# First stage of a two-block transformer kernel: scale, spreading of c and sums of squares moved to TensorE, first weights laid out by input block

## Chip, cores and metric

The kernel runs as one program on one core of a Trainium2 chip. The metric is the time of one execution on the device in microseconds (us); the span of a profile runs from its first to its last instruction.

## What is computed

A first block of two layers runs over x (512 positions by 1024 features), then a second block of two layers over the result. Only the start and the end matter here. Each sublayer of the first block normalises x and modulates it by vectors that come from c; the gated feed-forward network follows:

```python
def rmsnorm(x, g):
    y = xf * lax.rsqrt(jnp.mean(xf * xf, axis=-1, keepdims=True) + EPS)
    return y * g
def modulate(x, g, shift, scale):
    return rmsnorm(x, g) * (1.0 + scale[:, None, :]) + shift[:, None, :]
def first_block(...):
    c_act = jax.nn.silu(c)
    mod = (c_act @ w_mod[l] + b_mod[l]).reshape(c.shape[0], N_MOD, D_MODEL)
    h = modulate(x, g_norm[l, 0], mod[:, 0], mod[:, 1])
    x = x + 0.5 * mod[:, 2][:, None, :] * swiglu(h, w_ffn1_gu[l], w_ffn1_down[l])
    ...
```

The second block is modulated in the same way by vectors from c_2 and c_ctx_2, and its last step is a layer norm (mean and variance over the features) of the sum of x and the last feed-forward network; its result is the output.

## The kernel before, in words

**Layout.** x lies transposed: eight tiles of 128 features by 512 positions. A matrix product of fp32 accuracy is made of three fast ones (fp32r): each operand is split into a high half (a cast on ScalarE: wh, hh) and the rest (a subtraction on VectorE: wl, hl), and `mm3` issues high x high, high x low and low x high. A weight block is 128 x 512 (four tiles of 128 x 128, 256 KB); `wblk` loads it (wr) and makes wh and wl. `wcol` takes two blocks, all eight input tiles of one output tile.

**Order of work.** The program is first recorded, operation by operation, with a number each (`Recorder.call`: `prio` is the count of operations so far plus `later`). `Recorder.schedule` then plays all five queues with a cost per instruction (`Recorder.cost`) and lets each engine take the ready operation with the lowest number; the order that comes out is emitted. Loads all go through SyncE's queue and are ordered in the same way. A tag bounds what is under way: at most 8 weight blocks between load and split, 12 between load and last matmul, 8 PSUM banks.

**Start.** `setup` loads the eight x tiles, then `load_c(0, "c")` loads c twice 512 wide, broadcast by the DMA to 128 partitions, and ScalarE applies silu (b_c). `first_mods` makes the shift Sh and the scale G of the first sublayer, one feature chunk m of 128 at a time. Of wmod, transposed on the host so that a row belongs to one output feature, it loads two halves of 128 x 512 for the shift and two for the scale (mr). The dot product with b_c is one VectorE instruction with a running sum for one half of each; for the other half (`FIRST_POOL`) GpSimd multiplies and ScalarE sums. Small VectorE steps add the halves, the bias and the gain. `nc.later = FIRST[0] + FIRST[1] * m` moves the numbers of chunk m by 100 + 16 m; a chunk has 13 operations.

`rms` squares the x tiles on ScalarE (sq), adds the eight tiles on VectorE (`total`, seven adds), sums over partitions by four one-column fp32 matmuls with ones (`colsum`), takes the inverse root by ten small VectorE steps (`rsqrt`) and spreads the row over partitions by four transposes (`bcast`). `modulated` makes for each k: tm (VectorE), hh (ScalarE), hl (VectorE). Then `ffn` goes over pairs p of gate and value: for each of two halves eight input tiles k, 24 matmuls of 512 columns into a PSUM bank, then silu, product and split. `gu_blocks` packs the weights so that a block holds four input tiles of one output tile.

`setup_rest`, recorded after four steps of the first block, calls `load_c` for c_2 and the context's c (b_c2, b_cc). `run` interleaves the main line with `gen_mods`, which makes all other modulation vectors.

**End.** `ln_part` of the last layer (mod is None) works on two halves of 256 positions. Each sums x over the tiles on GpSimd and the squares on VectorE, sums both over partitions by two one-column matmuls each (`colsum`), makes mean and inverse root, spreads them (bm and a PSUM bank), and subtracts, multiplies and stores. The second half's is recorded behind all dense matmuls of the last down projection.

Names in the profile: mr (rows of wmod), b_c, sq, acc (sums of tiles), ones, c (small columns), mods (Sh and G), tm, hh/hl, wr/wh/wl, ps (any PSUM bank). Every operation shows line 446, the place where the planner emits it.

Of the kernel before, what the change touches and what calls it, by code (L numbers as in the profile page):

```python
# [40 lines left out]

def down_blocks():
    return [[(k, m) for m in range(m0, m0 + 4 // len(ch)) for k in ch] for ch in FF_CHUNKS for m0 in range(0, KD, 4 // len(ch))]
# [21 lines left out]
FIRST_POOL = (1, 3)  # L65
# [87 lines left out]
class Recorder:  # L153
# [28 lines left out]
    def cost(self, eng, method, a, k):  # L182
        out = a[0]
        n = out.width() if isinstance(out, View) else a[1].width()
        if eng == "tensor":
            if method == "transpose":
                return 0.84 * n + 2
            x = a[2]
            return max(0.4167 * n, 107) + 13.4 if x.t.dt == F32R else 112
# [281 lines left out]
class Core:  # L471
# [45 lines left out]
    def setup(self):  # L517
# [9 lines left out]
        self.cb = {}  # L527
        self.x = []
# [4 lines left out]
        self.load_c(0, "c")  # L533
# [7 lines left out]
    def load_c(self, i, k):  # L541
        nc = self.nc
        for h in range(2):
            t = self.t(s="b_" + k)
            nc.sync.dma_start(t, self.io["cvec"][i:i + 1, h * 512:(h + 1) * 512].to_broadcast([P, 512]))
            nc.scalar.activation(t, t, AF.Silu)
            self.cb[k, h] = t
# [95 lines left out]
    def first_mods(self):  # L643

        nc = self.nc
        Sh, G = self.mods[:, 0:8], self.mods[:, 8:16]
        for m in range(8):
            nc.later = FIRST[0] + FIRST[1] * m
            dots = []
            for ch in range(2):  # L650
                d = [self.col(1), self.col(1)]
                for h in range(2):
                    raw = self.t(s="mr")
                    nc.sync.dma_start(raw, self.io["wmod"][0, ch * 8 + m][:, h * 512:(h + 1) * 512])
                    if (2 * ch + h) % 4 in FIRST_POOL:
                        nc.gpsimd.tensor_tensor(raw, raw, self.cb["c", h], op=ALU.mult)
                        nc.scalar.activation(raw, raw, AF.Identity, accum_out=d[h])
                        continue
                    nc.vector.scalar_tensor_tensor(raw, raw, 1.0, self.cb["c", h], op0=ALU.mult, op1=ALU.mult, accum_out=d[h])
                dots.append(d)  # L660
            for ch, out in enumerate((Sh, G)):
                nc.vector.scalar_tensor_tensor(out[:, m:m + 1], dots[ch][0], dots[ch][1], self.bmod[:, ch * 8 + m:ch * 8 + m + 1], op0=ALU.add, op1=ALU.add)
            nc.vector.scalar_tensor_tensor(G[:, m:m + 1], G[:, m:m + 1], 1.0, self.gn[:, m:m + 1], op0=ALU.add, op1=ALU.mult)
# [63 lines left out]
    def colsum(self, tiles, T, eng=None, more=0):  # L727
        nc = self.nc
        acc = self.total(tiles, T, eng)
        st = self.ps()  # L730
        for j in range(T // P):
            nc.tensor.matmul(st[:, j:j + 1], acc[:, j * P:(j + 1) * P], self.ones, start=True, stop=True)
# [29 lines left out]
    def rms(self, x, T, width, eps=1e-6):  # L762
# [6 lines left out]
        st, v, q = self.colsum(sq, T, more=2)  # L769
# [24 lines left out]
    def ffn(self, x, h, gu, dn, gate, T, conv=None, before_last=None, head=HEAD, after=None):  # L794
        nc = self.nc
        last = len(FF_CHUNKS) - 1
        for ci, ch in enumerate(FF_CHUNKS):
            hid = []
            for pi, p in enumerate(ch):
                halves = []  # L800
                for half in range(2):
                    ws = self.wcol(gu, 2 * p + half)
                    pg = self.ps()[:, :T]
                    self.lin(pg, ws, h, parts=parts(T) if ci == 0 and 2 * pi + half < head else None)
# [22 lines left out]
        yield from self.ffn_end(x, dn, prev, hid, gate, T, after)  # L827

# [68 lines left out]
    def rms_part(self, l, sub):  # L897
# [3 lines left out]
        def part(sl):  # L901
# [4 lines left out]
            self.modulated(x, self.rms(x, T, D), G, Sh, [(hi[:, sl], lo[:, sl]) for hi, lo in out], T)  # L906
# [305 lines left out]
    def ln_part(self, xs, T, l, which, kind, mod, perm=False):  # L1212
# [8 lines left out]
        def part(sl):  # L1221
# [13 lines left out]
            s1 = self.colsum(x, C, nc.gpsimd)  # L1235
            s2, v, q = self.colsum(sq, C, more=2)
# [499 lines left out]
def layout(i):  # L1736
# [7 lines left out]
    o["wmod"] = np.stack([rowtiles(i["w_mod"][l]) for l in range(DEPTH)])  # L1744
    o["wada"] = np.stack([rowtiles(i["ada_w_2"][l]) for l in range(DEPTH)])
# [24 lines left out]
    for l in range(DEPTH):  # L1770
        o[f"gu1_{l}"] = pack(i["w_ffn1_gu"][l], gu_blocks())
# [70 lines left out]
```

## Time and profile before

| | before |
|---|---|
| median of 3 runs | 3553.25 us (3552.89 to 3555.09) |
| the profiled execution | 3556.54 us |
| its span | 3554.8 us |
| TensorE matmul, busy share | 97% |
| VectorE, ScalarE, GpSimd, busy share | 75%, 51%, 22% |
| share of the chain that ended last: TensorE, VectorE, ScalarE, DMA | 88%, 5%, 3%, 2% |
| TensorE busy in the first and the last of 40 slices | 6 and 8 tenths |

A slice is 88.9 us. Busy shares are averages over the whole span; in a window each column gives the busy time of an engine and, in brackets, its instructions. A matmul's own duration is longer than the distance to the next, because matmuls overlap: distances between starts tell the rate. An fp32 matmul (not fp32r) makes two records in the trace.

### The profile page before, as it was taken

What the parts mean: (1) busy time and instruction counts of PE and PEld (TensorE: products, weight loads), DVE (VectorE), ACT (ScalarE), POOL (GpSimd) and SP (SyncE); (2) the same over time, 40 slices, a digit from 0 to 9 for tenths busy, and PEclk for the clock granted to TensorE, in tenths of its full rate; (3) what the DMA queues carried; (4) which work ended last, traced back from release to release, by engine and by line L of the source; (5) the groups of instructions that cost most, each with busy time, mean ns of one, the idle gap of its engine ahead of it and who ended that gap; (6) DMA issues with size and microseconds to landing.
All of it is one profiled execution on the core that took longest, in us unless ns stands there. A gap on an engine that the chain in (4) does not pass through costs nothing.

```text
span 3554.8 us, 56919 instructions
## 1 busy us (share of the span) xinstructions
PE 3463.3 (97%) x19814; PEld 3046.3 (86%) x19814; DVE 2668.0 (75%) x5556; ACT 1811.8 (51%) x3933; POOL 768.6 (22%) x848
## 2 busy tenths in 40 slices
PE   6999999999999999999999999999999999989998
PEld 5888989888988889898888988888888889988887
DVE  8984689867697658798645699987668767876566
ACT  6443555534555455664333487874445444454333
POOL 4330032322132112223100133350001522240002
PEclk9999999999999999999999999999999999999999
DMA  9874145556376542448535212124343143333330
GB/s 337 293 229 123 58 151 155 184 159 191 104 252 193 163 119 93 117 146 268 180 104 150 87 44 60 57 69 130 106 127 107 54 125 104 91 105 104 97 90 24
DMA packets 276448, 475.37 MB, mean 134 GB/s; under 512 B 40000, under 2 KB 55872, under 8 KB 276160
## 3 DMA queue, kind: packets, MB, share of 16 engines
q1 hardware_dynamic: 276160, 471.74, 43.4%
q8 instruction: 156, 2.56, 0.3%
q14 instruction: 132, 1.08, 0.1%
HBM read 448.81 MB, written 5.50 MB: 128 GB/s over the span
## 4 chain that ended last, share of the span: by engine, by line
PE 88%; DVE 5%; ACT 3%; DMA 2%; issue 1%; POOL 0%; SPq 0%; POOLq 0%; DVEq 0%; ACTq 0%
PE ps L446 88%; DVE wl L446 1%; ACT L446 1%; DVE c L446 0%; DVE x L446 0%; DVE pl L446 0%; ACT pth L446 0%; ACT pl L446 0%; SPq L446 0%; DMA mr<-in_wmod 0%; DVE ptl L446 0%; ACT gt L446 0%; DMA wr<-in_dn 0%; DVE mr L446 0%; ACT pc L446 0%
## 5 line engine op out<-in xcount | busy, mean ns | idle before, releaser
L446 DVE TENSOR_TENSOR wl<-wr,wh 128x512 fp32r<-128x512 f32 (+1 forms) x1182 | 851.9, 741 | 136.8 <-ACT wh L446 100.7
L446 ACT CAST wh<-wr 128x512 fp32r<-128x512 f32 (+1 forms) x1182 | 678.5, 614 | 116.6 <-PE ps L446 65.5
L446 PE MATMUL ps<-hh,wh 128*128 128x512 f32 (+1 forms) x1864 | 687.7, 369 | 4.9 <-ACT hh L446 4.8
L446 PE MATMUL ps<-hh,wl 128*128 128x512 f32 (+1 forms) x1864 | 684.5, 367 | 6.0 <-DVE wl L446 6.0
L446 PE MATMUL ps<-hl,wh 128*128 128x512 f32 (+1 forms) x1864 | 685.4, 368 | 4.4 <-DVE hl L446 4.4
L446 PE MATMUL ps<-fh,wh 128*128 128x512 f32 (+1 forms) x1344 | 464.1, 345 | 0.0
L446 PE MATMUL ps<-fl,wh 128*128 128x512 f32 (+1 forms) x1344 | 461.8, 344 | 0.0
L446 PE MATMUL ps<-fh,wl 128*128 128x512 f32 (+1 forms) x1344 | 461.7, 344 | 0.0
L446 PEld LDWEIGHTS ps<-hh,wl 128*128 128x128 f32 x1864 | 352.2, 189 | 65.6 <-DVE wl L446 7.8
L446 PEld LDWEIGHTS ps<-hh,wh 128*128 128x128 f32 x1864 | 352.6, 189 | 61.7 <-ACT hh L446 5.8
L446 PEld LDWEIGHTS ps<-hl,wh 128*128 128x128 f32 x1864 | 352.5, 189 | 61.2 <-DVE hl L446 6.4
L446 DVE SCALAR_TENSOR_TENSOR x<-ps,mods,x 128x512 f32<-128x512 f32 (+1 forms) x400 | 255.2, 641 | 177.8 <-PE ps L446 173.9
L446 PE MATMUL ps<-ah,wh 128*128 128x512 f32 (+1 forms) x1000 | 367.1, 367 | 2.0 <-ACT ah L446 2.0
L446 PE MATMUL ps<-al,wh 128*128 128x512 f32 (+1 forms) x1000 | 366.1, 366 | 0.2
L446 PE MATMUL ps<-ah,wl 128*128 128x512 f32 (+1 forms) x1000 | 365.7, 366 | 0.0
L446 PEld LDWEIGHTS ps<-fh,wl 128*128 128x128 f32 x1344 | 254.5, 189 | 30.2
L446 PEld LDWEIGHTS ps<-fh,wh 128*128 128x128 f32 x1344 | 254.6, 189 | 29.5
L446 PEld LDWEIGHTS ps<-fl,wh 128*128 128x128 f32 x1344 | 254.7, 190 | 29.3
L446 DVE SCALAR_TENSOR_TENSOR cv<-ps,ffc,cv 128x511 f32<-128x511 f32 (+1 forms) x264 | 172.6, 658 | 140.0 <-ACT cv L446 136.8
L446 POOL TENSOR_TENSOR mr<-mr,b_c 128x512 f32<-128x512 f32 x123 | 182.2, 1484 | 403.2 <-DMA mr<-in_wmod 287.8
L446 ACT ACTIVATE cv<-ps,ffc 128x512 f32<-128x512 f32 (+1 forms) x132 | 93.2, 708 | 323.5 <-PE ps L446 323.0
L446 ACT CAST fh<-s 128x512 fp32r<-128x512 f32 x132 | 81.9, 621 | 276.9 <-DVE s L446 276.9
(332 smaller groups left out, 6947.0 us busy)
## 6 DMA issues: line engine op xcount, KB each, us to landing
wr<-in_gu SPq DMA_DIRECT2D x352, 256.0 KB, 3.3
mr<-in_wmod SPq DMA_DIRECT2D x288, 256.0 KB, 4.4
wr<-in_fin SPq DMA_DIRECT2D x264, 256.0 KB, 2.7
mr<-in_wada SPq DMA_DIRECT2D x192, 256.0 KB, 3.6
wr<-in_dn SPq DMA_DIRECT2D x176, 256.0 KB, 3.1
wr<-in_fout SPq DMA_DIRECT2D x132, 256.0 KB, 2.7
wr<-in_win SPq DMA_DIRECT2D x64, 256.0 KB, 3.1
wr<-in_nqkv SPq DMA_DIRECT2D x48, 256.0 KB, 3.0
```

The source lines that it names most:

```text
L446: getattr(eng, method)(*a, **k)
```

## The change

It makes the first scale on TensorE: wscale is the scale's part of w_mod with 128 input features on the partitions; for each m eight fp32 matmuls with a weight tile of 128 x 128 and one column of silu(c) (ccol) accumulate in a column of one PSUM bank (sums), and one VectorE step makes G. The shift's two products stay on VectorE, both halves. GpSimd and ScalarE have no product of the first stage any more. c is loaded as two rows ahead of x and spread over 128 partitions by fp32 matmuls with a row of ones, for c and, in `setup_rest`, for the two others. `colsum(each=True)` drops the adds and accumulates one-column matmuls of every tile in PSUM: in the first `rms` (8 x 4 matmuls) and in the last half of the last layer norm, for x and for the squares (2 x 8 x 2). The first four gate and value tiles of the first network (pairs 0 and 1) are packed by input block: block k holds input tile k of all four, and `first_pairs` accumulates in four PSUM banks, k by k. The planner's cost of an fp32 matmul of 256 columns or more rises to 1.7 ns a column.

```diff
--- before.py
+++ after.py
@@ -39,6 +39,11 @@
     return [[(k, m) for k in range(k0, k0 + 4)] for p in range(NFF) for m in (p, NFF + p) for k0 in (0, 4)]
 
 
+def first_blocks():
+
+    return [[(k, m) for m in (0, NFF, 1, NFF + 1)] for k in range(KD)] + gu_blocks()[8:]
+
+
 def down_blocks():
     return [[(k, m) for m in range(m0, m0 + 4 // len(ch)) for k in ch] for ch in FF_CHUNKS for m0 in range(0, KD, 4 // len(ch))]
 
@@ -62,7 +67,6 @@
 FIRST = (100, 16)
 HEAVY = 0.5
 FILL, DEBT, STEP = 0.7, 5000.0, 500.0
-FIRST_POOL = (1, 3)
 ON_DVE, ON_DVE_LAST = 1, 1
 BEGIN = 20000.0
 POOLED = (1, 3)
@@ -186,7 +190,7 @@
             if method == "transpose":
                 return 0.84 * n + 2
             x = a[2]
-            return max(0.4167 * n, 107) + 13.4 if x.t.dt == F32R else 112
+            return max(0.4167 * n, 107) + 13.4 if x.t.dt == F32R else 112 if n < 256 else 1.7 * n
         if eng == "sync":
             rows = (out.box[1] - out.box[0]) if isinstance(out, View) else P
             return max(450, rows * n * 4 / 360)
@@ -525,12 +529,13 @@
         nc.vector.memset(mean, 1.0 / D)
         nc.scalar.copy(self.mean, mean)
         self.cb = {}
+        self.firsts = []
+        self.load_c(0, "c")
         self.x = []
         for m in range(KD):
             t = self.t(s="x")
             self.nc.sync.dma_start(t, self.io["xT"][m * P:(m + 1) * P, :])
             self.x.append(t)
-        self.load_c(0, "c")
         self.gn = self.load_const("gnorm")
         self.bmod = self.load_const("bmod")
         self.mods = self.cst([P, 264], "mods")
@@ -540,10 +545,16 @@
 
     def load_c(self, i, k):
         nc = self.nc
+        row = self.new("t", (1, 512), F32, "crow"), self.new("t", (1, 512), F32, "crow")
         for h in range(2):
+            nc.sync.dma_start(row[h], self.io["cvec"][i:i + 1, h * 512:(h + 1) * 512])
+        one = self.new("t", (1, P), F32, "one")
+        nc.vector.memset(one, 1.0)
+        for h in range(2):
+            p = self.ps()
+            nc.tensor.matmul(p, one, row[h], start=True, stop=True)
             t = self.t(s="b_" + k)
-            nc.sync.dma_start(t, self.io["cvec"][i:i + 1, h * 512:(h + 1) * 512].to_broadcast([P, 512]))
-            nc.scalar.activation(t, t, AF.Silu)
+            nc.scalar.activation(t, p, AF.Silu)
             self.cb[k, h] = t
 
     def setup_rest(self):
@@ -644,23 +655,25 @@
 
         nc = self.nc
         Sh, G = self.mods[:, 0:8], self.mods[:, 8:16]
+        up, c = self.col(8), self.col(8)
+        nc.sync.dma_start(c, self.io["ccol"])
+        nc.scalar.activation(c, c, AF.Silu)
+        nc.vector.tensor_scalar(up, self.bmod[:, 8:16], 1.0, None, op0=ALU.add)
+        sums = self.ps()
         for m in range(8):
             nc.later = FIRST[0] + FIRST[1] * m
-            dots = []
-            for ch in range(2):
-                d = [self.col(1), self.col(1)]
-                for h in range(2):
-                    raw = self.t(s="mr")
-                    nc.sync.dma_start(raw, self.io["wmod"][0, ch * 8 + m][:, h * 512:(h + 1) * 512])
-                    if (2 * ch + h) % 4 in FIRST_POOL:
-                        nc.gpsimd.tensor_tensor(raw, raw, self.cb["c", h], op=ALU.mult)
-                        nc.scalar.activation(raw, raw, AF.Identity, accum_out=d[h])
-                        continue
-                    nc.vector.scalar_tensor_tensor(raw, raw, 1.0, self.cb["c", h], op0=ALU.mult, op1=ALU.mult, accum_out=d[h])
-                dots.append(d)
-            for ch, out in enumerate((Sh, G)):
-                nc.vector.scalar_tensor_tensor(out[:, m:m + 1], dots[ch][0], dots[ch][1], self.bmod[:, ch * 8 + m:ch * 8 + m + 1], op0=ALU.add, op1=ALU.add)
-            nc.vector.scalar_tensor_tensor(G[:, m:m + 1], G[:, m:m + 1], 1.0, self.gn[:, m:m + 1], op0=ALU.add, op1=ALU.mult)
+            for h in range(2):
+                raw = self.t(s="mg")
+                nc.sync.dma_start(raw, self.io["wscale"][m][:, h * 512:(h + 1) * 512])
+                for j in range(4):
+                    nc.tensor.matmul(sums[:, m:m + 1], raw[:, j * P:(j + 1) * P], c[:, 4 * h + j:4 * h + j + 1], start=h == 0 and j == 0, stop=h == 1 and j == 3)
+            nc.vector.scalar_tensor_tensor(G[:, m:m + 1], sums[:, m:m + 1], up[:, m:m + 1], self.gn[:, m:m + 1], op0=ALU.add, op1=ALU.mult)
+            d = [self.col(1), self.col(1)]
+            for h in range(2):
+                raw = self.t(s="mr")
+                nc.sync.dma_start(raw, self.io["wmod"][0, m][:, h * 512:(h + 1) * 512])
+                nc.vector.scalar_tensor_tensor(raw, raw, 1.0, self.cb["c", h], op0=ALU.mult, op1=ALU.mult, accum_out=d[h])
+            nc.vector.scalar_tensor_tensor(Sh[:, m:m + 1], d[0], d[1], self.bmod[:, m:m + 1], op0=ALU.add, op1=ALU.add)
         nc.later = 0
         self.mcol["w", 0, 0] = Sh
         self.mcol["w", 0, 1] = G
@@ -724,12 +737,15 @@
         eng.tensor_tensor(acc, sums[0], sums[1], op=ALU.add)
         return acc
 
-    def colsum(self, tiles, T, eng=None, more=0):
-        nc = self.nc
-        acc = self.total(tiles, T, eng)
+    def colsum(self, tiles, T, eng=None, more=0, each=False):
+
+        nc = self.nc
+        accs = tiles if each else [self.total(tiles, T, eng)]
+        n = len(accs)
         st = self.ps()
-        for j in range(T // P):
-            nc.tensor.matmul(st[:, j:j + 1], acc[:, j * P:(j + 1) * P], self.ones, start=True, stop=True)
+        for i, acc in enumerate(accs):
+            for j in range(T // P):
+                nc.tensor.matmul(st[:, j:j + 1], acc[:, j * P:(j + 1) * P], self.ones, start=i == 0 and j == 0, stop=i == n - 1 and j == T // P - 1)
         n = T // P
         return st[:, :n] if not more else tuple(st[:, i * n:(i + 1) * n] for i in range(more + 1))
 
@@ -759,14 +775,14 @@
 
         self.nc.gpsimd.tensor_scalar(p, p, c, 1.0, op0=ALU.mult, op1=ALU.mult)
 
-    def rms(self, x, T, width, eps=1e-6):
+    def rms(self, x, T, width, eps=1e-6, each=False):
         nc = self.nc
         sq = []
         for a in x:
             q = self.t(s="sq")[:, :T]
             nc.scalar.activation(q, a, AF.Square)
             sq.append(q)
-        st, v, q = self.colsum(sq, T, more=2)
+        st, v, q = self.colsum(sq, T, more=2, each=each)
         nc.vector.tensor_scalar(v, st, eps * width, None, op0=ALU.add)
         return self.bcast(self.rsqrt(v, width, q), T)
 
@@ -799,9 +815,12 @@
             for pi, p in enumerate(ch):
                 halves = []
                 for half in range(2):
-                    ws = self.wcol(gu, 2 * p + half)
-                    pg = self.ps()[:, :T]
-                    self.lin(pg, ws, h, parts=parts(T) if ci == 0 and 2 * pi + half < head else None)
+                    if gu == "gu1_0" and p < 2:
+                        pg = self.first_pairs(gu, h)[2 * p + half]
+                    else:
+                        ws = self.wcol(gu, 2 * p + half)
+                        pg = self.ps()[:, :T]
+                        self.lin(pg, ws, h, parts=parts(T) if ci == 0 and 2 * pi + half < head else None)
                     if conv is not None:
                         halves.append(self.conv3(pg, conv + (half * NFF + p) * 4, T))
                     else:
@@ -826,6 +845,15 @@
                 prev = hid
         yield from self.ffn_end(x, dn, prev, hid, gate, T, after)
 
+    def first_pairs(self, gu, h):
+
+        if not self.firsts:
+            self.firsts = [self.ps() for _ in range(4)]
+            for k in range(KD):
+                for pg, w in zip(self.firsts, self.wblk(gu, k)):
+                    self.mm3(pg, w, h[k], k == 0, k == KD - 1)
+        return self.firsts
+
     def ffn_end(self, x, dn, prev, hid, gate, T, after):
 
         gate = self.mod(*gate)
@@ -903,7 +931,7 @@
             G = self.mod("w", l, 3 * sub + 1)
             T = sl.stop - sl.start
             x = [a[:, sl] for a in self.x]
-            self.modulated(x, self.rms(x, T, D), G, Sh, [(hi[:, sl], lo[:, sl]) for hi, lo in out], T)
+            self.modulated(x, self.rms(x, T, D, each=T == S), G, Sh, [(hi[:, sl], lo[:, sl]) for hi, lo in out], T)
             yield from ()
 
         return out, part
@@ -1232,8 +1260,8 @@
                 q = self.t(s="sq")[:, :C]
                 nc.scalar.activation(q, a, AF.Square)
                 sq.append(q)
-            s1 = self.colsum(x, C, nc.gpsimd)
-            s2, v, q = self.colsum(sq, C, more=2)
+            s1 = self.colsum(x, C, nc.gpsimd, each=not mod and sl.start > 0)
+            s2, v, q = self.colsum(sq, C, more=2, each=not mod and sl.start > 0)
             mu, m2 = self.col(n), self.col(n)
             nc.vector.tensor_scalar(mu, s1, 1.0 / D, None, op0=ALU.mult)
             nc.vector.scalar_tensor_tensor(m2, s1, -1.0, mu, op0=ALU.mult, op1=ALU.mult)
@@ -1742,6 +1770,8 @@
     o["gnorm"] = np.concatenate([cols(i["g_norm"].reshape(-1)), cols(i["g_final"])], 1)
     o["bmod"] = np.concatenate([cols(i["b_mod"][0]), cols(i["b_mod"][1]), cols(i["ada_b_2"][0]), cols(i["ada_b_2"][1])], 1)
     o["wmod"] = np.stack([rowtiles(i["w_mod"][l]) for l in range(DEPTH)])
+    o["wscale"] = i["w_mod"][0][:, D:2 * D].reshape(KD, P, KD, P).transpose(2, 1, 0, 3).reshape(KD, P, D)
+    o["ccol"] = cols(i["c"][0])
     o["wada"] = np.stack([rowtiles(i["ada_w_2"][l]) for l in range(DEPTH)])
     pairs = [0, 4, 1, 5, 2, 6, 3, 7]
     o["sinks"] = np.repeat(i["attn_sinks"][:, pairs], 2, axis=1).reshape(1, 32)
@@ -1768,7 +1798,7 @@
                     lrug[l, 64 * e:64 * e + 64, c0:c0 + 64] = w[l, 2 * t + e]
     o["lrug"] = lrug
     for l in range(DEPTH):
-        o[f"gu1_{l}"] = pack(i["w_ffn1_gu"][l], gu_blocks())
+        o[f"gu1_{l}"] = pack(i["w_ffn1_gu"][l], gu_blocks() if l else first_blocks())
         o[f"gu2_{l}"] = pack(i["w_ffn2_gu"][l], gu_blocks())
         o[f"dn1_{l}"] = pack(i["w_ffn1_down"][l], down_blocks())
         o[f"dn2_{l}"] = pack(i["w_ffn2_down"][l], down_blocks())
```

## Rows read from the trace of the kernel before

**Rows 1.** Windows: busy time by engine (instructions), granted clock, DMA share, GB/s
```profile
core 0: us, PE busy (x) PEld busy (x) DVE busy (x) ACT busy (x) POOL busy (x), PEclk, DMA share, GB/s
21.00:60.00 39.00, 28.23 (x104) 20.43 (x105) 38.89 (x71) 26.00 (x58) 18.27 (x13) 1.00 1.02 358
60.00:120.00 60.00, 59.90 (x265) 49.32 (x264) 59.88 (x133) 28.79 (x60) 18.61 (x13) 1.00 0.88 298
3500.00:3539.00 39.00, 39.00 (x316) 38.42 (x314) 25.56 (x57) 11.00 (x23) 15.41 (x21) 1.00 0.09 28
```

**Rows 2.** Waits of TensorE, 0 to 60 us: total, times, longest
```profile
PE ps L446 <- DVE acc L446: 11.5, 1, 11.5
PE ps L446 <- DVE wl L446: 6.0, 4, 3.8
PE ps L446 <- ACT hh L446: 4.0, 2, 3.4
PE ps L446 <- DVE hl L446: 3.7, 3, 1.8
```

**Rows 3.** By tile (mr, mods), 12 to 62 us: VectorE, ns min/median/max, first and last start
```profile
L446 DVE SCALAR_TENSOR_TENSOR mr<-mr,b_c x18: 675/680/1767, 13.5 to 61.0; 128x512 f32<-128x512 f32 x18
L446 DVE SCALAR_TENSOR_TENSOR mods<-c,c,bmod x14: 204/208/1333, 16.7 to 60.2; 128x1 f32<-128x1 f32 x14
L446 DVE SCALAR_TENSOR_TENSOR mods<-mods,gnorm x7: 143/149/1270, 18.3 to 60.9; 128x1 f32<-128x1 f32 x7
L446 DVE SCALAR_TENSOR_TENSOR tm<-x,mods,ps x7: 732/746/748, 19.6 to 61.6; 128x512 f32<-128x512 f32 x7
L446 DVE SCALAR_TENSOR_TENSOR hl<-tm,mods,hh x6: 739/742/1766, 23.2 to 55.9; 128x512 fp32r<-128x512 f32 x6
```

**Rows 4.** Timeline of TensorE in the first stage: start us, us
```profile
11.54 1.87 PE L446 MATMUL ps<-ones,acc 128*128 128x1 f32 x8 [11.54 <-DVE acc L446]
...
28.61 0.80 PE L446 MATMUL ps<-hh,wl 128*128 128x512 f32 x1 [3.83 <-DVE wl L446]
29.21 0.63 PE L446 MATMUL ps<-hh,wh 128*128 128x512 f32 x1
29.64 0.63 PE L446 MATMUL ps<-hl,wh 128*128 128x512 f32 x1
...
31.72 0.39 PE L446 MATMUL ps<-hh,wh 128*128 128x512 f32 x1
31.95 0.39 PE L446 MATMUL ps<-hl,wh 128*128 128x512 f32 x1
```

**Rows 5.** Timeline of SyncE's queue, DMA issues: start us, us
```profile
0.74 3.71 SPq L446 DMA_DIRECT2D x<-in_xT  x8
4.49 1.21 SPq L446 DMA_DIRECT2D b_c<-in_cvec  x2
...
7.27 6.56 SPq L446 DMA_DIRECT2D mr<-in_wmod  x10
14.11 0.33 SPq L446 DMA_DIRECT2D wr<-in_gu  x1
...
43.10 1.02 SPq L446 DMA_DIRECT2D b_c<-in_cvec  x2
```

**Rows 6.** By tile (wr), 0 to 62 us: cast, low half, landing
```profile
L446 ACT CAST wh<-wr x18: 602/605/626, 20.1 to 55.4; 128x512 fp32r<-128x512 f32 x18
L446 DVE TENSOR_TENSOR wl<-wr,wh x16: 675/680/1770, 27.9 to 60.3; 128x512 fp32r<-128x512 f32 x16
...
DMA to landing us min/median/max: 2.6/5.4/5.9
```

**Rows 7.** Timeline of TensorE: fp32 transposes of 128 columns in a full stretch
```profile
3105.18 1.91 PE L446 MATMUL ps<-ident,P 128*128 128x128 f32 x16
3106.85 0.36 PE L446 MATMUL ps<-pth,V 128*128 128x256 f32 x1
```

**Rows 8.** Timeline of TensorE: sums of the last layer norm's two halves
```profile
3523.42 0.95 PE L446 MATMUL ps<-ones,acc 128*128 128x1 f32 x8
3524.23 0.36 PE L446 MATMUL ps<-fh,wh 128*128 128x256 f32 x1
...
3538.99 0.28 PE L446 MATMUL ps<-fh,wl 128*128 128x256 f32 x1
3541.58 1.05 PE L446 MATMUL ps<-ones,acc 128*128 128x1 f32 x8 [2.31 <-POOL acc L446]
```

**Rows 9.** Timeline of VectorE: the sums of the last half are read
```profile
3542.22 0.16 DVE L446 TENSOR_SCALAR c<-ps 128x2 f32<-128x2 f32 x1 [0.42 <-PE ps L446]
```

**Rows 10.** Windows: granted clock behind the last sums
```profile
3543.00:3545.00 2.00, 0.00 (x0) 0.00 (x0) 1.86 (x8) 0.31 (x1) 1.61 (x3) 0.74 0.00 0
```

## The prediction

> **What bounds the kernel now.** I read the windows first, by stage, then TensorE's waits and its timeline in the stages that are not full, then the queues that feed them. From 60 us on TensorE is full: 265 matmuls in 60 us are 0.226 us each, and they wait for nothing [rows 1]. Before that, 104 matmuls of 512 columns fill 104 x 0.226 = 23.5 us of 60, so the first stage loses 36.5 us. Whatever the change does there is worth the difference in that loss, since later work on TensorE only moves along with it. The waits name the losers: 11.5 us until the sum of squares, then the low halves of the weights (wl) and the two halves of h, which VectorE makes [rows 2]. VectorE is busy 38.89 of 39 us there, partly by stretching: hl takes 0.742 us in the median and up to 1.766, a product of mr 0.680 and up to 1.767, a one-column step 0.208 and up to 1.333 [rows 1, 3]. GpSimd multiplies beside it. The other full stage is the end: 39 of 39 us busy up to 3539, then a chain of single steps [rows 1].
>
> The clock is told by pitch: 512 columns every 0.43 us from 29.21, every 0.23 us from 31.72; these are 1.2 and 2.4 GHz [rows 4]. The granted clock reads 1.00 over all of it [rows 1], so it does not show the low start. Dense work from 28.61 on preceded the rise.
>
> **First stage, when the dense stream can start.** SyncE issues in the order of the planner's numbers. Before, chunk m of the scale and shift has loads from 100 + 29 m, and the first weight block has 162 (8 x 13 + 34 for sums, root and spreading + 24 for h), so ten loads precede it; the timeline shows just that: ten, then one block at 14.11 [rows 5]. After, a chunk has 16 operations, so its loads start at 100 + 32 m; the first block has 128 + 55 (sums, root, spreading) + 24 (h) = 207. All of m = 0, 1, 2 and three loads of m = 3 precede it: 15. Ten loads took from 7.27 to 14.11, 0.68 us each; five more put the block's issue at 17.5. It lands 5.4 us later and its cast takes 0.605 [rows 6]: first dense matmul at about **23.5 us**. The start of the loads themselves hardly moves: two rows of c come ahead of x (two issues of 0.46 us) and ccol is one more, while two broadcast loads of 1.21 us go [rows 5]. The bytes are the same: wscale and the new block order only lay them out differently.
>
> What TensorE has to do before 23.5 us: c is spread by two fp32 matmuls, which the trace before does not have. A sum of squares shows that an fp32 matmul makes two records (eight for four matmuls, [rows 4]); a transpose of 128 fp32 columns takes (3106.85 - 3105.18)/16 = 0.104 us [rows 7], so 512 columns twice are 8 x 0.104 = 0.84 us, at the low clock 1.7. Lower bound 0.23, the rate of the dense stream. Then 32 one-column sums of squares and 4 x 8 for the scale of m = 0 to 3. A one-column matmul costs (3524.23 - 3523.42)/4 = 0.20 us at the high clock [rows 8] and about 0.45 at the low one (four in 1.87 us less the end of the last, [rows 4]). At the high clock: 3.4 (the spreading, still low) + 6.4 + 6.4 + 0.4 for four transposes of the roots = 16.6 us from about 3.4 us (issue at 0.74, shortest landing 2.6, [rows 5, 6]), so done by 20.0: hidden under the wait for weights. I take the high clock: 3.4 us of 512-column work is as much as preceded the rise at 31 us.
>
> From 23.5 on TensorE is the bound. The 96 matmuls of the first two pairs and those of pair 2 behind them follow the h tiles; between them lie the scale sums of m = 4 to 7, 32 x 0.20 = 6.4 us. Does VectorE keep up? Per chunk two products and wl at 0.68, tm and hl at 0.746 and 0.742, and small steps of 0.208 and 0.149: 3.9 us [rows 3, 6]; eight chunks 31.1, the root's ten small steps 2. From 12.7 us on (first load issued at 7.27, 5.4 to land) that ends at 45.8; with 0.3 of stretching left in each chunk, at 48.2. TensorE needs the last h tile only at 23.5 + 7 x 12 x 0.226 + 6.4 = 49 us. So the VectorE work is covered. What leaves VectorE, ScalarE and GpSimd (seven adds, 16 GpSimd products, 16 ScalarE sums, eight small ones) makes that cover and is worth nothing more. If it does not relieve VectorE and its stretching stays, TensorE waits as before and the gain is gone (the third rival). New waits: each scale column holds VectorE's queue until its eight matmuls are done, with products behind it; that is inside the 3 us of slack. Loss after: 23.5 + 6.4 = 29.9 against 36.5: **-6.6 us**. Bounds: -13.0 if the one-column matmuls cost nothing beside dense ones, +7.5 at the low clock (below).
>
> **The two later vectors.** c2 and the context's c are spread the same way: four fp32 matmuls of 0.84 = **+3.4 us** on TensorE. Their loads went out at 43.1 us [rows 5], in the stretch that I have just called full, so I take them whole; between 0 (a gap) and 3.4. They save four transfers, which nothing waits for.
>
> **The end.** In the last half of the last layer norm, 2 x 8 tiles x 2 = 32 one-column matmuls replace four. The planner numbers them behind all dense matmuls of that half, and the dense stream has no gap, so 28 run after 3538.99 with the last tile's four. 32 x 0.20 = 6.4 us; before, the sums were read at 3542.22, 3.2 us after the stream [rows 8, 9]. **+3.2 us**. The other bound is the wait for GpSimd's adds gone, -2.31 [rows 8]. I take +3.2, since these rows are that very place.
>
> **Sum:** -6.6 + 3.4 + 3.2 = 0.0. The profiled execution took 3556.54 us (span 3554.8) and stands 3.3 us above the median; from the median, 3553.2. About 0.2%, 7.1 us, is what can be told from no change.
>
> **Rivals.**
> *The clock does not hold* (slower). If one-column matmuls do not keep the high clock, the work before the stream is 3.4 + 32 x 0.45 + 32 x 0.45 + 0.8 = 33.0 us from 3.4, so the stream begins at 36.4 instead of 23.5, and at the low rate for some 2.5 us (29.21 to 31.72 [rows 4], 1.2 lost). Loss 36.4 + 1.2 + 6.4 = 44.0: +7.5, and with 3.4 and 3.2 the time is 3553.2 + 14.1 = 3567.3; if half of the early sums still run fast, 3563. It decides as soon as TensorE's early work passes 20 us, that is, at over about 0.25 us per one-column matmul. For it: a sum and a transposition at the end did not hold the clock: it fell in the window 3543 to 3545 (0.74 on the mean), 2 us after the last sums began [rows 8, 10], and the only one-column sums at the start ran slow [rows 4]. Against it: four sums are a short burst after an idle stretch, not a stream.
> The Trainium skill, "TensorE: Matmul & The Clock Gate", section on HAM oscillation, describes bursts of matmuls that wait for transfers between them and fall back to the half rate every time. The scale sums are such bursts, eight per chunk behind their loads; by that rule the time is this rival's, not mine. The fall at the end agrees with it (0.74); that one-column work counts as too little is shown by no row here.
>
> *The one-column matmuls hide* (faster). Their cost is weight loading, and PEld runs beside PE. If the loads are taken under the dense matmuls, the 6.4 us go, c2's spreading falls in gaps, and the end gains up to 2.3: loss 23.5, -13.0 - 2.3 = -15 at most, 3538; with the eight of a chunk standing in a row and hiding half, about -10, 3543. Against it: the eight records at 3523.42 stood between dense matmuls and still took 0.81 us [rows 8].
>
> *It does not do what it says*: TensorE starts with h as before because VectorE is still late. Then only +6.6 remain: 3560. This lies within my range and I count it half to no change, half to the slow rival.
>
> **How the numbers follow.** My forecast, gains and costs that cancel, has 0.45: no change. The low clock has 0.35: slower. Hidden matmuls have 0.20: faster. The likeliest time is 3553.2; its own range 3546 to 3560. For 8 in 10 the range must take in most of the slow rival and the half-hidden case: 3543 to 3568.
>
> **What would show it.** Right: the first block is issued after 15 loads at about 17.5 us; the first dense matmul stands at 23 to 25 with a pitch of 0.23 from the start; one-column matmuls in the first 20 us have a pitch of 0.10 per record; about 60 - 29.9 = 30 us of dense work, 133 matmuls of 512 columns, lie before 60 us; four 0.84 us matmuls somewhere at 45 to 80 us; the end's sums last until 3545 on the scale of before. Wrong: records of one column at 0.22 us with the stream from 35 us on (slow rival), or eight of them inside the dense pitch (fast rival), or VectorE as the releaser of TensorE's waits after 30 us.

## The result and the profile after

| | before, on the same chip | after |
|---|---|---|
| median | 3554.17 us (3552.89 to 3560.12) | 3578.11 us (3577.25 to 3580.12) |
| ratio, 95% interval | | 1.0063 [1.0051, 1.0076] |
| profiled execution, its span | 3556.54, 3554.8 us | 3578.78, 3577.0 us |
| first product of fh (`ps<-fh,wh`) starts | 91.19 | 109.40 |
| last product of fh starts | 3538.99 | 3556.20 |
| from there to the end of the span | 15.8 | 20.8 |

The change is slower by 24 us, beyond the forecast of no change and 10 us beyond the range. The landmarks say where. The first product of fh stands behind 240 dense matmuls of hh and hl (three groups of 80 by line and tile) in after, and behind the same ones in before, so its start tells how long the first stage took: +18.2 us. The last product of fh is 17.2 us late, so the 3.4 ms between give or take 1.0. The end is 5.0 us longer. 18.2 - 1.0 + 5.0 = 22.2 us, the difference of the spans.

TensorE's timeline of after, the first stage up to where the dense stream runs at full rate (start us, duration us, records of one kind in a row, in brackets the idle time and its releaser):

```profile
2.24 3.74 PE L450 MATMUL ps<-crow,one 1*128 1x512 f32 x4 [2.24 <-DMA crow<-in_cvec]
7.19 13.81 PE L450 MATMUL ps<-ones,sq 128*128 128x1 f32 x64 [1.21 <-ACT sq L450]
20.86 3.55 PE L450 MATMUL ps<-c,mg 128*128 128x1 f32 x16
24.72 3.58 PE L450 MATMUL ps<-c,mg 128*128 128x1 f32 x16 [0.31 <-DVE mods L450]
...
37.53 0.77 PE L450 MATMUL ps<-hh,wh 128*128 128x512 f32 x1
...
40.21 0.63 PE L450 MATMUL ps<-hl,wh 128*128 128x512 f32 x1
40.63 0.63 PE L450 MATMUL ps<-hh,wl 128*128 128x512 f32 x1
...
42.17 0.40 PE L450 MATMUL ps<-hh,wh 128*128 128x512 f32 x1
42.41 0.39 PE L450 MATMUL ps<-hl,wh 128*128 128x512 f32 x1
```

To be seen: 64 one-column records take 13.81 us, 0.216 each, so a one-column fp32 matmul (two records) costs 0.43 and not 0.20. TensorE hardly waits, it is simply busy until 37.53, and then the dense matmuls still have a pitch of 0.43 until 42.17, where it becomes 0.23.

The same timeline further on, at the last scale sums and at the spreading of c2 and cc:

```profile
70.09 1.95 PE L450 MATMUL ps<-c,mg 128*128 128x1 f32 x16 [0.31 <-DVE mods L450]
72.35 0.53 PE L450 MATMUL ps<-hh,wh 128*128 128x512 f32 x1 [0.31 <-DVE mods L450]
72.68 0.63 PE L450 MATMUL ps<-hl,wh 128*128 128x512 f32 x1
73.11 0.63 PE L450 MATMUL ps<-hh,wl 128*128 128x512 f32 x1
...
76.09 0.40 PE L450 MATMUL ps<-hh,wh 128*128 128x512 f32 x1
...
92.88 0.39 PE L450 MATMUL ps<-hh,wl 128*128 128x512 f32 x1
93.20 3.90 PE L450 MATMUL ps<-crow,one 1*128 1x512 f32 x8
97.03 0.80 PE L450 MATMUL ps<-hh,wh 128*128 128x512 f32 x1
97.62 0.63 PE L450 MATMUL ps<-hl,wh 128*128 128x512 f32 x1
98.05 0.63 PE L450 MATMUL ps<-hh,wl 128*128 128x512 f32 x1
```

On two occasions the pitch doubles again behind work that is not dense: after the scale sums (16 records in 1.95 us, so still at the high clock) and after the eight records of one row. The windows name the clock (length, busy us of each engine with its instructions, granted clock, DMA share, GB/s):

```profile
core 0: us, PE busy (x) PEld busy (x) DVE busy (x) ACT busy (x) POOL busy (x), PEclk, DMA share, GB/s
7.20:20.80 13.60, 13.60 (x64) 13.60 (x65) 0.17 (x1) 4.19 (x8) 0.00 (x0) 1.00 0.94 330
72.00:76.00 4.00, 3.69 (x10) 2.93 (x10) 3.92 (x11) 3.31 (x8) 0.57 (x1) 0.58 0.37 125
96.00:100.00 4.00, 4.00 (x10) 2.46 (x9) 4.00 (x10) 2.82 (x7) 0.99 (x1) 0.57 0.91 299
3559.00:3561.00 2.00, 2.00 (x20) 2.00 (x19) 0.32 (x2) 0.00 (x0) 0.00 (x0) 1.00 0.00 0
3561.00:3566.00 5.00, 5.00 (x25) 4.75 (x24) 0.31 (x2) 0.00 (x0) 0.00 (x0) 0.51 0.00 0
```

0.58 and 0.57 are mixtures of 1.00 and 0.50, that is of 2.4 and 1.2 GHz. The first row reads 1.00 although its pitch is the low one, as [rows 1] did for before: up to the first change of the clock the column shows nothing.

The end of after, TensorE's timeline:

```profile
3556.32 3.63 PE L450 MATMUL ps<-ones,x 128*128 128x1 f32 x32
3559.81 5.81 PE L450 MATMUL ps<-ones,sq 128*128 128x1 f32 x32
3565.48 0.67 PE L450 MATMUL ps<-ident,c 128*128 128x128 f32 x2
```

The first 32 records run at 0.11. In the second 32 the clock falls at about 3561, with TensorE busy without a gap, and they take 5.81 us.

What the prediction expected on the other side did happen. TensorE's waits in after, 0 to 130 us (total, times, longest), and SyncE's queue:

```profile
PE ps L450 <- DMA crow<-in_cvec: 2.2, 1, 2.2
PE ps L450 <- DVE mods L450: 1.6, 5, 0.3
PE ps L450 <- ACT sq L450: 1.2, 1, 1.2
PE ps L450 <- DVE wl L450: 0.5, 1, 0.5
```

```profile
18.29 0.33 SPq L450 DMA_DIRECT2D wr<-in_gu  x1
```

The 25.2 us of waits in [rows 2] (28.7 with one of 3.5 us for VectorE's `c`, which those rows leave out) are 5.5 us, VectorE's part of them 2.1, and the first weight block goes out behind 15 loads, at 18.29 for the predicted 17.5.

**The first stage's loss added up.** The 240 dense matmuls ahead of the landmark take 240 x 0.226 = 54.2 us at the full rate; what the landmark stands beyond that is lost. Before it is 37.0 us, 36.5 of them up to 60 us, as the prediction has it. After it is 55.2: 37.5 until the stream begins; 2.6 for nine dense matmuls from 37.53 to 42.17 (4.64 - 9 x 0.226), 0.45 of it a wait for wl; 7.8 for the scale sums inside the stream with two waits of 0.31 us (72 dense matmuls stand between 48.30 and 72.35); 1.7 for the nine from 72.35 to 76.09; 3.9 from where the matmul after 92.88 was due (93.11) to 97.03, and 1.5 for the seven from there to 100.10.

### The profile page after: what moved, and what is told of

Its sections match the earlier page's. It is cut to its first block, busy times and chain, and to the rows that moved or that the text cites. A ratio compares the mean times of both kernels' runs of the same rounds, so it can differ in the third digit from the quotient of the medians.

```text
span 3577.0 us, 57361 instructions
## 1 busy us (share of the span) xinstructions
PE 3514.3 (98%) x20066; PEld 3095.1 (87%) x20066; DVE 2645.0 (74%) x5538; ACT 1800.4 (50%) x3902; POOL 734.7 (21%) x825
## 4 chain that ended last, share of the span: by engine, by line
PE 93%; DVE 3%; ACT 2%; DMA 1%; issue 1%; POOL 0%; SPq 0%; POOLq 0%; DVEq 0%; ACTq 0%
PE ps L450 93%; ACT L450 0%; DVE wl L450 0%; DVE x L450 0%; DVE ptl L450 0%; DVE c L450 0%; ACT pth L450 0%; ACT pl L450 0%; DMA wr<-in_win 0%; DVE pl L450 0%; ACT pc L450 0%; ACT wh L450 0%; DMA kc<-kc 0%; ACT Qh L450 0%; DVE os L450 0%
## 5 line engine op out<-in xcount | busy, mean ns | idle before, releaser
L450 POOL TENSOR_TENSOR mr<-mr,b_c 128x512 f32<-128x512 f32 x107 | 154.2, 1441 | 437.9 <-DMA mr<-in_wmod 230.1
```

Of the source, the lines that this page charges most:

```text
L450: getattr(eng, method)(*a, **k)
```

## The experiments

Each runs beside the kernel before on the same chip; the ratio is to that. "First fh" is the landmark of the table. Two traces of equal code gave 90.06 and 91.06 us for it (below), and the work from there to the last product of fh takes 3443 to 3449 us in all these kernels, before (3447.8) and after (3446.8) among them; so the first stage is judged by the landmark and not by the median alone. Every edit also lets the planner order all operations anew, so a part can move others. Its new cost of long fp32 matmuls was not undone by itself.

**One part of the change undone at a time.** First the end (`ln_part` without `each`):

```
-            s1 = self.colsum(x, C, nc.gpsimd, each=not mod and sl.start > 0)
-            s2, v, q = self.colsum(sq, C, more=2, each=not mod and sl.start > 0)
+            s1 = self.colsum(x, C, nc.gpsimd)
+            s2, v, q = self.colsum(sq, C, more=2, each=False)
```

> The changed kernel with the sums of the last half of the last layer norm as before (GpSimd and VectorE add, four one-column matmuls). Theory 1 (one-column matmuls let the clock fall and run at 1.2 GHz): from the last dense matmul to the end 15.8 us as before instead of 20.8, so 5.0 us less than the changed kernel, about 3573. Theory 2 (only their number counts, 0.20 us each): 3.2 us less, about 3575. Theory 3 (the order shifted elsewhere): the end keeps its 20.8 us.

3573.27 us (3572.02 to 3575.61), ratio 1.0045 [1.0028, 1.0062]: 4.8 us back. The last product of fh starts at 3558.07 in a span of 3573.5, 15.4 us from the end. Its sums wait 2.31 us for GpSimd's adds and then take 1.05 us for eight records, in place of 9.2 us for 64:

```profile
3560.65 1.05 PE L450 MATMUL ps<-ones,acc 128*128 128x1 f32 x8 [2.31 <-POOL acc L450]
```

Then the later spreading (c2 and cc by broadcast loads, the first c still by TensorE):

```
-        self.load_c(1, "c2")
-        self.load_c(2, "cc")
+        self.load_cb(1, "c2")
+        self.load_cb(2, "cc")
```

> The changed kernel with the two later vectors (c2 and the context's c) loaded by broadcast transfers as before; the first c is still spread by TensorE. Theory 1 (they stand in the full stream and let the clock fall behind them): 3.8 us of matmuls and 1.2 us of low pitch go, 5 us less, about 3573. Theory 2 (only their 0.85 us each): 3.4 us less, about 3575. If they sit in a gap: no change.

3574.2 us (3572.35 to 3576.59), ratio 1.0049 [1.0034, 1.0064]; first fh at 104.95, 4.5 us earlier. The eight records and the slow matmuls behind them are worth 3.9 + 1.5 = 5.4 by the sum above; 4.5 came back. The rest went at the start, where the clock rises later: the 13th dense matmul starts at 43.72 instead of 42.86.

Then the first sums of squares (seven adds on VectorE and four matmuls as before):

```
-            self.modulated(x, self.rms(x, T, D, each=T == S), G, Sh, ...
+            self.modulated(x, self.rms(x, T, D, each=False), G, Sh, ...
```

> The changed kernel with the first sums of squares as before (seven adds on VectorE, four one-column matmuls); the scale stays on TensorE. Theory 1 (TensorE's early one-column work at 1.2 GHz is the path): 28 of 32 matmuls at 0.43 us go, of which some 4 us had to wait for x anyway: the dense stream starts at 28 to 30 us instead of 37.5, 8 us less, about 3570. Theory 2 (at 0.20 us each): 28 of them are 5.6 us, most of it under the loads of x: 0 to 2 us less. Theory 3 (weights or VectorE hold the stream): no change.

3569.99 us (3568.71 to 3575.92), ratio 1.004 [1.0025, 1.0055]; first fh at 104.41. The stream begins at 28.03, 9.5 us earlier, but only 5.0 are left at the landmark. Its timeline shows where the rest went:

```profile
59.90 1.84 PE L450 MATMUL ps<-c,mg 128*128 128x1 f32 x16
62.05 3.57 PE L450 MATMUL ps<-c,mg 128*128 128x1 f32 x16 [0.31 <-DVE mods L450]
...
86.57 4.44 PE L450 MATMUL ps<-crow,one 1*128 1x512 f32 x8
```

The clock falls between the two last chunks of the scale rather than behind them, so the second takes 3.57 instead of 1.95 us, and the spreading costs more as well. In these two traces it is a matter of timing which burst meets the fall.

Then the scale (products on VectorE and GpSimd as before):

```
-                for j in range(4):
-                    nc.tensor.matmul(sums[:, m:m + 1], raw[:, j * P:(j + 1) * P], c[:, 4 * h + j:4 * h + j + 1], ...
+                    if (2 * ch + h) % 4 in FIRST_POOL:
...
+                    nc.vector.scalar_tensor_tensor(raw, raw, 1.0, self.cb["c", h], ... accum_out=d[h])
```

> The changed kernel with scale and shift made as before (two halves on VectorE, two on GpSimd and ScalarE); sums of squares, spreading of c and the block order stay. Theory 1: 36 one-column matmuls ahead of the stream go, about 14.5 us on TensorE; the stream starts at 23 to 25 us, with VectorE late again behind it; first stage 8 to 14 us shorter, about 3564 to 3570. Theory 3 (the order by input block starves TensorE): the stream has gaps as in the kernel before or longer ones and the time stays at 3575 or more.

3570.42 us (3570.07 to 3570.93), ratio 1.0039 [1.0024, 1.0053]; first fh at 98.67, 10.7 us earlier, the largest of the four. The first dense matmul starts at 27.88 instead of 37.53, but the third follows only at 35.84, 3.4 us sooner than in after (39.19), for VectorE is the bound again (TensorE's timeline, and its waits, 0 to 100 us):

```profile
27.88 0.80 PE L451 MATMUL ps<-hh,wh 128*128 128x512 f32 x1 [2.72 <-ACT wh L451]
...
35.84 0.80 PE L451 MATMUL ps<-hh,wl 128*128 128x512 f32 x1 [4.45 <-DVE wl L451]
...
51.03 2.84 PE L451 MATMUL ps<-crow,one 1*128 1x512 f32 x6
```

```profile
PE ps L451 <- DVE wl L451: 6.1, 2, 4.4
PE ps L451 <- DVE mods L451: 3.0, 1, 3.0
PE ps L451 <- DVE hl L451: 2.8, 2, 1.9
```

By place the 10.7 us are 3.3 of the sooner stream, 9.5 of the scale sums inside it and the low clock behind them (7.8 + 1.7), and 1.3 of the spreading, less 3.4 of waits for VectorE inside the stream. The spreading moved: the planner puts it at 47.03 (two records) and 51.03 (six), and behind it the dense pitch stays 0.23, so it costs 4.1 us in place of 5.4. So the scale on TensorE does relieve VectorE as predicted, and costs more than it relieves.

**One part alone.** The kernel before with only the order of the first four blocks (`first_blocks`, `first_pairs`) changed, the hunks being those of the change:

> The kernel before with one part of the change alone: the weights of pairs 0 and 1 by input block, four PSUM banks filled k by k. Theory 1 (TensorE's early small matmuls made the change slow): this part by itself costs nothing and may start the stream earlier, since one h tile feeds twelve matmuls: 3546 to 3554. Theory 3 (the block order starves TensorE, because each k waits for its own VectorE steps): slower than before, 3558 to 3570.

3554.12 us beside 3557.12, ratio 0.999 [0.9981, 1.0]; first fh at 90.06. In more rounds:

> The kernel before with only the order of the first four blocks changed, measured again in more rounds. Theory 1 (eight matmuls for each h tile that arrives, in place of a wait for all, take a microsecond out of the first stage): 3551 to 3554 us, ratio 0.9990 to 0.9997. Theory 2 (its first comparison was scatter): ratio 1.0000 within 0.0005.

3553.46 us, ratio 0.9991 [0.9982, 1.0], first fh at 91.06. The block order costs nothing. (One tile of h feeds twelve matmuls, four banks with three products each, not eight.) Whether it gains is not settled: the landmark moved by 1.1 and 0.1 us, the rest of the difference lies in the 3.4 ms behind it, where nothing was changed.

**Dense work between the one-column matmuls.** The changed kernel with one unread dense matmul behind each early one-column one:

```
+                if T == S and each:
+                    self.dense()      # fp32r, 128x512, into a bank that nobody reads
...
+                    if m < 4:
+                        self.dense()
```

> The changed kernel with more work: behind each of the 32 one-column matmuls of the first sums and of the 32 scale matmuls of chunks 0 to 3 stands one dense matmul of 512 columns (fp32r, constant operands) into a PSUM bank that nobody reads. Theory 1 (the clock is low because one-column work does not hold it): the clock rises within the sums, a one-column record takes 0.10 us instead of 0.22, 64 x (0.20 + 0.23) is 27.5 us as 64 x 0.43 was, the stream starts at 36 to 39 us as before this edit and at full rate at once: within 3 us of the changed kernel. Theory 2 (the records have that length whatever the clock): 64 x 0.23 to 0.43 us more ahead of the stream, 15 to 27 us slower, 3593 to 3605.

3590.28 us (3588.4 to 3592.97), ratio 1.0096 [1.0081, 1.0111]: 12.2 us slower than after, which is neither number; first fh at 124.11, 14.7 later, which is what the 64 dense matmuls take by themselves (64 x 0.226 = 14.5). The planner did not alternate them throughout, and that is what makes the trace useful:

```profile
7.92 2.78 PE L450 MATMUL ps<-fill 128*128 128x512 f32 x11
10.54 1.84 PE L450 MATMUL ps<-ones,sq 128*128 128x1 f32 x16
...
33.98 3.54 PE L450 MATMUL ps<-fill 128*128 128x512 f32 x8
37.36 0.28 PE L450 MATMUL ps<-c,mg 128*128 128x1 f32 x2
37.50 0.48 PE L450 MATMUL ps<-fill 128*128 128x512 f32 x1
37.82 0.28 PE L450 MATMUL ps<-c,mg 128*128 128x1 f32 x2
```

```profile
13.00:37.00 24.00, 24.00 (x97) 22.35 (x96) 5.80 (x26) 0.62 (x1) 0.00 (x0) 0.51 1.02 376
37.00:47.00 10.00, 10.00 (x62) 8.78 (x62) 2.83 (x11) 0.00 (x0) 0.00 (x0) 0.99 0.96 353
```

Behind dense fillers (from 2.79 us on, the last eleven at a pitch of 0.24) the same sums of squares run at 0.106 per record (10.54 to 12.24), where they took 0.216 in after: the cost of a one-column matmul is the clock's, not the place's. From about 13 to 37 us TensorE is busy all the time and the clock is 0.51; it comes back behind eight dense matmuls in a row (33.98). From 37.36 to 46 it stays at 0.99, with fillers and sums in turn and twelve fillers in a row at 40.91. So the low clock can be avoided, but a pair of filler and sum then takes 0.46 us (37.36 to 37.82), and the sum alone at the low clock 0.43: filling buys nothing.

**Three parts undone at once**, the end, the later spreading and the first sums, so that the scale, the first c and the block order are left (the first three diffs above together):

> The changed kernel with three of its parts undone at once: the sums at the end, the sums of squares of the first stage and the spreading of c2 and cc are as before. Left are the first scale by one-column matmuls, the first c spread by TensorE and the order of the blocks. Theory 1 (each part costs its own time, and they add): the first product of fh starts at 109.4 - 4.5 - 5.0 = 99.9 us, the end comes 15.7 us after the last of fh, and the time is 3578.1 - 4.8 - 4.5 - 5.0 = 3563.8 us; the 8.7 us that the first product of fh is then behind before's 91.2 are the price of the scale. Theory 2 (the parts share one loss, the low clock, so that taking one away lets another have it): the first product of fh stays at 103 us or later, and the time is 3567 us or more. Theory 3 (the early sums were what kept TensorE low, and without them the scale hides in its idle time): at 95 us or sooner, 3559 us or less.

3560.69 us (3557.28 to 3562.84), ratio 1.0012 [1.0003, 1.0021]; first fh at 95.08:

```profile
27.75 0.77 PE L450 MATMUL ps<-hh,wh 128*128 128x512 f32 x1
...
61.15 1.95 PE L450 MATMUL ps<-c,mg 128*128 128x1 f32 x16 [0.31 <-DVE mods L450]
...
64.08 0.63 PE L450 MATMUL ps<-hh,wl 128*128 128x512 f32 x1
64.51 0.63 PE L450 MATMUL ps<-hh,wh 128*128 128x512 f32 x1
```

Expected by adding the parts: 99.9; measured 14.3 us in place of 9.5, at the border of theory 3. The 14.3 is the earlier start (37.53 to 27.75 is 9.8) and the spreading's 4.5: both whole this time, because the fall of the clock stands behind the last scale sums, as in after, and not within them, as when the sums alone were undone. The time is likewise 3 us below the addition. What is left against before, 95.08 - 91.19 = 3.9 us, is the price of the three remaining parts together. The scale's own share is not isolated: with the block order and the first c but without the scale (the next run) the landmark stands at 93.42, 1.7 us sooner, and equal code differs by 1.0.

**Two attempts to use the idle time.** The kernel before with the block order and the first c spread by TensorE:

> The kernel before with the new block order and the first c spread by TensorE (two matmuls of one row by 512 columns) in place of two broadcast loads. Theory 1 (it stands in TensorE's idle time, and c is there long before the first products): the first product of fh within 1 us of 90.1, time within 2 us of the block order alone. Theory 2 (the two rows ahead of x on SyncE put off the squares and with them all of h by the 0.9 us of two issues, with no gain against it): 91 us or later. Theory 3 (the spreading raises the clock early, and the first dense matmuls run at 0.23 at once): 89 us or sooner, pitch 0.23 from the first dense matmul.

3554.95 us, ratio 1.0 [0.9991, 1.0009]; first fh at 93.42, 2.4 to 3.4 later than the block order alone. That is theory 2's time, but its reason is not shown. The sum of squares does start late, at 14.29 instead of 11.4 to 12.2 (TensorE waits for VectorE's `acc`), yet nothing is lost by it up to the 36th dense matmul, which starts at 38.08 against 37.99 and 38.03 with the block order alone. The time goes behind it, at the fourth tile of h, for which TensorE waits until 44.43; with the block order alone it goes on at 40.46 and 40.26:

```profile
44.43 0.79 PE L451 MATMUL ps<-hh,wh 128*128 128x512 f32 x1 [5.96 <-ACT hh L451]
```

Why that tile comes so late stays open. The first dense matmuls have the low pitch, so whatever the spreading at 2.30 did to the clock, it was of no use to them.

And with the block order and the scale of m = 0 and 1 alone on TensorE:

```
+            if m < 2:
+                for h in range(2):
...
+                        nc.tensor.matmul(sums[:, m:m + 1], raw[:, j * P:(j + 1) * P], c[:, 4 * h + j:4 * h + j + 1], ...
-            for ch in range(2):
+            for ch in range(1 if m < 2 else 2):
```

> The kernel before with the new block order and, of the change's other parts, only the scale of m = 0 and 1 on TensorE (16 one-column matmuls); the other six chunks are multiplied on VectorE and GpSimd as before. Theory 1 (one-column work costs only where it lasts past the first dense matmul): 16 x 0.43 = 6.9 us lie between 11.5 and 19 us, where TensorE has nothing else, VectorE is relieved of two products and GpSimd of two, and the first product of fh starts at 88 to 90 us (90.1 with the block order alone): 3551 to 3553 us. Theory 2 (what decides is where the loads and VectorE's later steps stand, not two products): 90 to 92 us and no difference. Theory 3 (one-column work before the stream hurts wherever it stands, since it delays the rise of the clock): 93 us or later, 3556 us or more.

3552.82 us (3550.6 to 3555.03), ratio 0.9989 [0.998, 0.9998]; first fh at 91.16, which is theory 2. Its 32 slow records end at 22.06, where the first dense matmul stood with the block order alone (22.07, and 21.23 in the second trace). They cost nothing that the landmark shows, and nothing is gained in that stage either. What theory 3 feared is there but small: the dense pitch becomes 0.23 at 33.59 instead of 32.06 and 32.33, and later waits for VectorE take that up.

```profile
13.27 3.55 PE L451 MATMUL ps<-c,mg 128*128 128x1 f32 x16
...
18.78 3.41 PE L451 MATMUL ps<-c,mg 128*128 128x1 f32 x16
```

It is the fastest kernel of the study, some 25 us below after and 0.1% below before, but as with the block order alone the difference to before does not lie where the change is, so no cause is shown for it.

## Why the prediction was wrong

The step that failed is the one that said "I take the high clock: 3.4 us of 512-column work is as much as preceded the rise at 31 us." Neither half held.
- The spreading (2.24 to 5.98) did not raise the clock: the records behind it take 0.216 us. Nor did it hold it later: from 93.20 eight such records end in a low pitch. It is 512 columns long like a dense matmul, but its stationary operand has one row. The rows of before showed dense work of 128 rows ahead of the rise [rows 4], and I took its length alone as the likeness. With dense fillers from 2.79 us on, the same spreading between them, the records behind run at 0.106.
- One-column matmuls neither raised it nor held it for long: from 7.19 to 37.5 TensorE is busy but for waits of 0.31 us, at the low clock all through; at the end the clock falls within such a stream, 4.7 us after the last dense matmul.

No run separates the single column, the single row and the type (fp32, where the dense work is fp32r): which of them it is stays open.

The slow rival had the mechanism (one column at 0.45, measured 0.43; stream at 36.4, measured 37.5) and its own deciding point, 0.25 us per matmul, was passed. It got 0.35, since I read the fall at the end of before [rows 8, 10] as the work of an idle stretch. Its time, 3567.3, is still 11 us short, in good part because it had the low clock at the start alone. By place, its terms against the measured ones: loss until the stream and the low start behind it 37.6, measured 40.1; scale sums in the stream 6.4, measured 7.8 with two of the five waits of 0.31 us (for `mods`, VectorE's step that reads the column before from the same bank, a new wait that I had not listed; three stand ahead of the stream) and 1.7 of low clock; spreading 3.4, measured 5.4 with the low clock behind it; end 3.2, measured 5.0. That is 2.5 + 3.1 + 2.0 + 1.8 = 9.4, less the 1.0 us of the middle and 0.5 that before lost between 60 us and the landmark: 7.9 of the 8.1 by which the spans differ more than 14.1. The rest of the 11 is what executions differ by.

What was right: 15 loads ahead of the first weight block; the block order and byte counts neutral; VectorE no longer the bound of the first stage, so the third rival did not happen; one-column matmuls do not hide under dense ones, so the fast rival did not either (eight records between dense matmuls at 68.83 took 0.95 us). The term of -6.6 became +13.1 with the scale sums' own waits and low clock (36.5 against 37.5 + 2.6 + 7.8 + 1.7 = 49.6). That sign is most of the error; the other two terms were 2.0 and 1.8 us too small.

The Trainium skill, "TensorE: Matmul & The Clock Gate", section on HAM oscillation, was cited for bursts that fall back while they wait for transfers. It pointed the right way, but not for its reason here: the fall at 72 us comes behind waits of 0.31 us, and those within the eight records from 93.20 and at 3561 behind none.

## What to carry to other kernels

Before work is moved to an idle TensorE, ask what clock it will run at: here one-column and one-row fp32 matmuls that stood by themselves ran at the low clock for 30 us, and amid dense work the longest rows of them left the low clock to the dense matmuls behind. Price them by the low rate (0.43 us for one column here) and count them only where they end before dense work could start, as 16 matmuls did here and 66 did not. A part's price under a clock that rises and falls is not additive, so measure combinations as well as single parts. And look at what the planner believes: in all these kernels it prices a one-column fp32 matmul at 112 ns, about a quarter of the 0.43 us measured, and an order made with the measured price was not run.

## What was not expected of the hardware

- TensorE busy for 13.60 of 13.60 us with one-column fp32 matmuls, and for some 30 us in all, stayed at 1.2 GHz; behind dense fillers the same matmuls ran at twice the rate (0.106 for 0.216 per record).
- Matmuls of 512 columns whose stationary operand is one row did not raise the clock at the start, and it was low after eight such records in a row (3.9 us).
- Not every such burst was followed by a fall: 16 one-column records amid dense work (1.84 us, at 41.71 and at 46.27 with three parts undone) and six one-row records (2.84 us, at 51.03 with the scale undone) were not; 24 one-column records with one wait of 0.31 us (from 68.83 in after) were.
- Alternating dense and one-column matmuls, with twelve dense ones in between, kept the high clock from 37.36 us on, yet at the low clock the same alternation, four pairs from 14.36 and four from 25.88, did not bring it back; it was back behind eight dense matmuls in a row (33.98 to 37.36).
